# The low halves of the weights: from a subtraction on VectorE to an accumulating DMA, in a two-layer decoder trunk

## The chip, the cores and the metric

One core of one Trainium2 chip runs the whole program. The metric is the device time of one execution in microseconds (us); lower is better. The kernel before takes 1878.02 us (median of 2 runs, 1877.92 to 1878.12).

## The reference

Two layers over 512 tokens of width 1024, all in float32. Cut to the products, since all the weights that the change speaks of are used in them:

```python
for l in range(DEPTH):                       # 2
    h = rmsnorm(x, norm_mix_g[l])
    proj = h @ w_in[l]                       # 1024 x 7328: latents, q/k/v of three branches, gates
    y_a = latent attention (w_uq, w_ukv); y_b = stick-breaking attention; y_c = retention
    up = jnp.einsum('bsnw,nwd->bsnd', branches, w_branch[l])
    gates = jax.nn.sigmoid(gate_logits.reshape(B, S, N_BRANCH, D_MODEL))
    x = x + jnp.einsum('bsnd,bsnd->bsd', gates, up) @ w_out[l]
    h = rmsnorm(x, norm_mlp_g[l])
    x = x + jnp.square(jax.nn.relu(h @ w_up[l])) @ w_down[l]   # 1024 x 4096, 4096 x 1024
return rmsnorm(x, final_norm_g)
```

## The kernel before, in words

**Three products for one.** TensorE takes its operands as float32r, a rounded float32. To keep float32 accuracy each weight is used as a sum of two float32r parts, `hi` (the weight rounded) and `lo` (the rest), and so is each activation. A product is three matmuls per slice of 128 rows: hi by hi, hi by lo and lo by hi. `mm_T` (lines 460 to 465) writes transposed outputs, 128 columns by 512 tokens: its matmuls have the lines 462, 463 and 464, and only line 464 reads the `lo` part of a weight. `mm_N` (lines 467 to 476) writes natural outputs, 128 tokens by 256 columns.

**Units of weights.** The class `Weights` streams all weights in the order of their use. A chunk (mostly 1024 rows by 256 columns, 1 MB) is one DMA on SyncE's queue (SP) into one of two buffers `raw` (line 86). A chunk holds two units of 128 partitions by 1024 numbers (512 KB). `split` makes the two parts of a unit: ScalarE (ACT) rounds the unit into a buffer `whi`, and VectorE (DVE) subtracts that from the raw unit into a buffer `wlo` (both line 104). There are four pairs of these buffers, `whi0` to `whi3` and `wlo0` to `wlo3`, used in turn. `pump` splits up to two units ahead of the one that is taken; when the last unit of a chunk is split, the next chunk is asked for. There are 292 units of this plain form (`form` is None); the units of `w_uq` and `w_ukv` have forms of their own and are split in small pieces.

A unit holds either 8 slices of 128 columns (`plan_T` with 1024 rows: rows of 512 bytes in DRAM) or 4 slices of 256 columns (`plan_N`, and the branch weights: rows of 1 KB). Either way TensorE works on it for 24 matmuls of 512 columns or as much as that.

**Order of the work.** In each layer: inputs of the stick-breaking attention, latents, retention's values; then dense products with an attention in between (stick-breaking, latent, retention), since a driver interleaves the attentions' steps with the dense tiles; then the output projection (`w_out`, 8 units) and the MLP: four groups of 8 units of `w_up` and 8 of `w_down`. In the last group of the second layer the `w_down` tiles are computed in two halves of 256 tokens, so that its 8 units are streamed twice and each is used for half as long (16 half units, `put_last`, lines 1305 to 1321). The program's scheduler puts each engine's instructions in an order before the run; each engine then works in that order.

**GpSimd (POOL)** has little to do: the loads of constants, a power for each normalisation (lines 417 and 1032), the reload of the residual in front of the output projection (line 1229) and its store at the end of a layer (line 1300), which are DMAs on POOL's queue.

Of the kernel before, what the change touches and what calls it, by code (L numbers as in the profile page):

```python
# [10 lines left out]
F32 = mybir.dt.float32  # L11
R = mybir.dt.float32r
I32 = mybir.dt.int32
AF = mybir.ActivationFunctionType
ALU = mybir.AluOpType
# [6 lines left out]
EPS = 1e-6  # L22
# [6 lines left out]
GATE_RUN = (2, 2, 4)  # tiles of gates before their branch products  # L29
SC = 96.0**-0.5  # L30

# columns of w_in
# [3 lines left out]
# columns of the constant pack  # L36
# [8 lines left out]
# rows of the gain pack  # L45
# [3 lines left out]
class Weights:  # L49
    """Streams weight chunks from DRAM and splits each unit into two float32r parts."""  # L50
# [16 lines left out]
    def chunk(self, srcs, k, cols, units):  # L67
        """srcs: list of (dram view [p, k, c], column); units: list of (k0, k1, c0, c1, form)"""
        c = len(self.chunks)
        self.chunks.append((srcs, k, cols))  # L70
        self.left.append(len(units))
        for u in units:
            self.units.append((c, u))
# [18 lines left out]
    def split(self):  # L92
        nc = self.nc
        u = self.n_split
        c, (k0, k1, c0, c1, form) = self.units[u]
        s = self.free.popleft()
        self.slot[u] = s
        self.n_split += 1
        src = self.raw(c)[:, k0:k1, c0:c1]
        nk, w = k1 - k0, c1 - c0  # L100
        if form is None:
            hi = self.his[s][:, : nk * w].rearrange("p (k c) -> p k c", c=w)
            lo = self.los[s][:, : nk * w].rearrange("p (k c) -> p k c", c=w)
            self.last = (nc.scalar.copy(hi, src).ins, nc.vector.tensor_sub(lo, src, hi.bitcast(F32)).ins)  # L104
        elif form == "kv":
            # [head, key | value, 64] to [key | value, head, 64]
            hi = self.his[s][:, : nk * w].rearrange("p (k c) -> p k c", c=w)
            lo = self.los[s][:, : nk * w].rearrange("p (k c) -> p k c", c=w)
            for k in range(nk):
                a = src[:, k].rearrange("p (h s d) -> p h s d", s=2, d=64)  # L110
                b = hi[:, k].rearrange("p (s h d) -> p h s d", s=2, d=64)
                nc.scalar.copy(b, a)
                nc.vector.tensor_sub(lo[:, k].rearrange("p (s h d) -> p h s d", s=2, d=64), a, b.bitcast(F32))
        else:
            # a head's 96 columns of w_uq, as [64 | 32 | 32 swapped] or [32 | 32 swapped | 64]
            w = 128
            hi = self.his[s][:, : nk * w].rearrange("p (k c) -> p k c", c=w)
            lo = self.los[s][:, : nk * w].rearrange("p (k c) -> p k c", c=w)
            if form == 0:
                parts = [(0, 0, 96), (96, 80, 16), (112, 64, 16)]  # L120
            else:
                parts = [(64, 0, 64), (0, 64, 32), (32, 80, 16), (48, 64, 16)]
            for dst, at, n in parts:
                nc.scalar.copy(hi[:, :, dst : dst + n], src[:, :, at : at + n])
            for dst, at, n in parts:
                nc.vector.tensor_sub(
                    lo[:, :, dst : dst + n], src[:, :, at : at + n], hi[:, :, dst : dst + n].bitcast(F32)
                )
        self.views = getattr(self, "views", {})
        self.views[u] = (hi, lo)  # L130
        self.left[c] -= 1
        if self.left[c] == 0:
            self.dma()
# [20 lines left out]
def trunk_kernel(  # L154
# [15 lines left out]
    nc = tc.nc  # L170
# [7 lines left out]
    # ---------------------------------------------------------------- buffers  # L178
# [36 lines left out]
    # the functions of one table set are issued together  # L215
# [11 lines left out]
    def table(out, in_, func, **kw):  # L227
        """an activation from the table set in use"""
        i = nc.scalar.activation(out, in_, func, **kw).ins
        tc.add_manual_dep(i, phase["first"].name, order, reason="table set")  # L230
        phase["all"].append(i)

    # ---------------------------------------------------------------- driver
# [24 lines left out]
    def lend():  # L258
        """between attentions their banks serve the dense products"""
        dt.extend(spare)  # L260
# [8 lines left out]
    def evacuate(ps, fn):  # L269
        """run fn a little later; then ps may be written again"""  # L270

        def go():
            fn()
            waiting[id(ps)] = False

        defer(go)
# [38 lines left out]
    # ---------------------------------------------------------------- weights  # L315
# [3 lines left out]
    def plan_T(ap, width=256):  # L319
        """columns for transposed outputs, in units of 128"""  # L320
        v = planes(ap, 0)
        nk, cols = v.shape[1], v.shape[2]
        for c in range(0, cols, width):
            w = min(width, cols - c)
            step = 1024 // nk
            W.chunk([(v[:, :, c : c + w], 0)], nk, w, [(0, nk, a, a + min(step, w - a), None) for a in range(0, w, step)])
# [53 lines left out]
    # ---------------------------------------------------------------- constants  # L380
# [30 lines left out]
    # per-token statistics -----------------------------------------------------  # L411
    def to_rstd(ms, n, width, power=-0.5):
        """(ms / n + EPS) ** -0.5 for a [128, width] sum of squares"""
        a = tiny()
        nc.vector.tensor_scalar(a[:, :width], ms, 1.0 / n, EPS, op0=ALU.mult, op1=ALU.add)
        r = tiny()
        nc.gpsimd.tensor_tensor(r[:, :width], a[:, :width], mhalf[:, :width], op=ALU.pow)
        return r

    def token_sums(parts, n=NT):  # L420
        """sums over the partitions of all parts [128, 128 n] as [128 tokens, n]"""
        ps = rot(tt)
        for t in range(n):
            for i, a in enumerate(parts):
                nc.tensor.matmul(
                    ps[:, t : t + 1], a[:, t * P : (t + 1) * P], ones, start=(i == 0), stop=(i == len(parts) - 1)
                )
        return ps[:, :n]

    def row_sums(ps, sq):  # L430
        """sums over the partitions of sq, on every partition"""
        nc.tensor.matmul(ps, ones.to_broadcast([P, P]), sq, start=True, stop=True)

    def spread_to(ps, r, n=NT):
        """ps[:, token] = r[token] on every partition"""
# [10 lines left out]
    def split_to(hi, lo, src, g=None):  # L446
        """hi + lo = src * g"""
# [7 lines left out]
    # products -----------------------------------------------------------------  # L455
    def mm_T(ps, wh, wl, xs):
        """ps [128 columns, 512 tokens]; wh, wl: per k [128, 128]; xs: per k (hi, lo)"""
# [9 lines left out]
    def mm_N(ps, wh, wl, xs, t):  # L467
        """ps [128 tokens, N]; wh, wl: per k [128, N]"""
# [13 lines left out]
    class Later:  # L482
        """parts that a deferred step still has to emit"""
# [12 lines left out]
    def tile_T(xs, evac):  # L496
        """the next unit of 128 columns"""
# [7 lines left out]
    def tiles_N(n_units, evac):  # L505
        """the next units, stacked along k, for every token tile"""
# [10 lines left out]
    # ---------------------------------------------------------------- attention  # L517
    flatA = aT.rearrange("p r c -> p (r c)")

    def put_A(i, e, ps):  # L520
        """store the transposed blocks j = 0..i of query tile i and parity e"""
# [16 lines left out]
    def mask(z, i, m):  # L538
        """mask the diagonal blocks of query tile i"""
# [44 lines left out]
    def stick_breaking(qT, kT, v, yb):  # L584
        def first(p, i):
# [9 lines left out]
            # a[t] = sigmoid(z[t]) * product over t' > t of sigmoid(-z[t'])  # L595
# [58 lines left out]
    def retention(l, rq, rk, rv, rg, yc):  # L654
# [28 lines left out]
        def scores(t):  # L683
            # within the chunk, [key, query]
# [19 lines left out]
        def outputs(t):  # L704
            c = st[t]
            y = c["y"] = rot(zt)[:, 0]
            for p in range(PAIRS):
                b = slice(p * P, (p + 1) * P)
                if t:
                    # the state is zero between a pair's heads  # L710
# [9 lines left out]
            if t < NT - 1:  # L720
                # state after the chunk
# [25 lines left out]
        def norms(t):  # L747
            # group norm and gate, natural layout
# [15 lines left out]
            # 2 * silu  # L764
# [42 lines left out]
    # ---------------------------------------------------------------- set-up  # L807
    def setup():
# [35 lines left out]
        def tables():  # L844
            """cos and sin of positions * frequencies"""
# [30 lines left out]
            # per token: cos cos | -sin sin, over sqrt(96)  # L876
# [8 lines left out]
    # ---------------------------------------------------------------- a layer  # L885
    def layer(l, box):
        """box['next']: per-token rstd [128, 4] of the layer's input, once known"""
# [18 lines left out]
        # ---- stick-breaking inputs  # L906
        sq, sk, sv, yb = {}, {}, [get() for _ in range(NT)], {}

        def put_q(p):
            # per head [hi | hi], and the lo parts of the pair  # L910
# [13 lines left out]
        def put_k(p):  # L924
            # per head [hi | lo] or [lo | hi]
# [68 lines left out]
        # ---- latent vectors  # L994
# [26 lines left out]
        def stat_c(key, n):  # L1021
            # the latents still lack their token's rstd, which this folds in
# [39 lines left out]
        # ---- latent attention inputs  # L1062
# [67 lines left out]
        # ---- gates and branches  # L1130
# [58 lines left out]
        # ---- retention inputs, rotated  # L1189
# [45 lines left out]
        # ---- output projection, residual  # L1235
        stats = {}

        def new_x(m, g):
            """xm[m] is final: square it, split it"""
# [26 lines left out]
        # ---- MLP  # L1266
# [92 lines left out]
    # ---------------------------------------------------------------- run  # L1359
# [10 lines left out]
def _constants():  # L1370
    """tables that depend on shapes alone"""
# [29 lines left out]
def _layout(inputs):  # L1401
    """the program's inputs, in its order: x by columns, the gains and positions by partitions"""
# [29 lines left out]
```

## Time and profile before

| | us |
|---|---|
| median of 2 runs | 1878.02 |
| span of the profiled execution, first to last instruction | 1875.9 |
| TensorE (PE) busy in it | 1857.7 (99%) |
| VectorE (DVE) busy | 1064.1 (57%) |
| ScalarE (ACT) busy | 717.4 (38%) |
| GpSimd (POOL) busy | 42.5 (2%) |

The profile is of one execution with a span of 1875.9 us, 2.1 us under the median of the runs; that difference is what lies around the first and last instruction and between executions. Busy times of different engines lie beside each other and do not add up. A matmul's record lasts longer than the step to the next one, since matmuls are pipelined; the pace of TensorE is read from how many start in a stretch.

### The profile page before, as it was taken

To read this page: it belongs to the slowest core of one execution; us is meant where nothing else is said; L and a number is where in the kernel's file an instruction comes from. 1 tells how busy PE (TensorE), PEld (TensorE's weight loads), DVE (VectorE), ACT (ScalarE), POOL (GpSimd) and SP (SyncE) were. 2 spreads that over 40 slices of the span, in tenths; PEclk is the share of its full clock that TensorE was granted. 3 is DMA by queue.
4 is the path that set the end of the run, shared out by engine and by line. 5 is a ranking of instruction groups with operands and counts; after the bars stand their busy time and mean duration, and the time that the engine had idled before them with its cause. 6 is when DMAs were issued, how large, how long until landed. Compare 5 with 4: busy or idle time off the path is not lost.

```text
span 1875.9 us, 23563 instructions
## 1 busy us (share of the span) xinstructions
PE 1857.7 (99%) x9668; PEld 1533.4 (82%) x9668; DVE 1064.1 (57%) x1706; ACT 717.4 (38%) x1191; POOL 42.5 (2%) x57
## 2 busy tenths in 40 slices
PE   8999999999999999999999999999999999999998
PEld 7878877988888888888897787779888888888887
DVE  6775566577555444444638647646764654444456
ACT  5555444233243222323436454432333432323244
POOL 1000000001000000000000000000010000000000
PEclk9999999999999999999999999999999999999999
DMA  5220132122432322332423112221224233223324
GB/s 182 83 86 25 48 100 79 57 69 89 132 104 93 107 93 90 96 105 92 129 76 102 46 36 80 68 88 59 79 90 135 90 99 104 90 90 103 100 92 133
DMA packets 163980, 169.81 MB, mean 91 GB/s; under 512 B 5920, under 2 KB 160048, under 8 KB 163872
## 3 DMA queue, kind: packets, MB, share of 16 engines
q1 hardware_dynamic: 161360, 160.97, 27.4%
q0 software_dynamic: 2368, 7.30, 1.2%
q8 instruction: 76, 1.25, 0.3%
q14 instruction: 32, 0.26, 0.0%
q10 hardware_dynamic: 144, 0.03, 0.0%
HBM read 164.09 MB, written 4.19 MB: 90 GB/s over the span
## 4 chain that ended last, share of the span: by engine, by line
PE 98%; DMA 1%; DVE 1%; issue 0%; ACT 0%; POOLq 0%; SPq 0%; DVEq 0%
PE d L462 24%; PE d L464 24%; PE d L463 24%; PE d L474 4%; PE d L475 4%; PE d L476 4%; PE t L556 3%; PE t L548 2%; PE z L627 2%; PE z L593 1%; PE z L592 1%; DMA raw<-in_w_in_dram 1%; PE z L715 1%; PE z L476 1%; PE z L475 1%; PE z L474 1%
## 5 line engine op out<-in xcount | busy, mean ns | idle before, releaser
L104 ACT CAST whi<-raw 128x1024 fp32r<-128x1024 f32 (+1 forms) x292 | 305.9, 1049 | 672.5 <-PE d L463 552.9
L104 DVE TENSOR_TENSOR wlo<-raw,whi 128x1024 fp32r<-128x1024 f32 (+1 forms) x292 | 354.9, 1216 | 222.2 <-ACT whi L104 221.2
L462 PE MATMUL d<-xh,whi 128*128 128x512 f32 x1072 | 425.5, 397 | 7.0 <-ACT whi L104 7.0
L464 PE MATMUL d<-xh,wlo 128*128 128x512 f32 x1072 | 420.7, 393 | 0.6 <-DVE wlo L104 0.5
L463 PE MATMUL d<-xl,whi 128*128 128x512 f32 x1072 | 421.1, 393 | 0.1
L462 PE MATMUL d<-slot,whi 128*128 128x512 f32 (+1 forms) x960 | 368.5, 384 | 0.3 <-DVE slot L1309 0.3
L464 PE MATMUL d<-slot,wlo 128*128 128x512 f32 (+1 forms) x960 | 362.6, 379 | 0.0
L463 PE MATMUL d<-slot,whi 128*128 128x512 f32 (+1 forms) x960 | 362.1, 379 | 0.0
L462 PEld LDWEIGHTS d<-xh,whi 128*128 128x128 f32 x1072 | 201.9, 188 | 51.8 <-ACT whi L104 7.5
L464 PEld LDWEIGHTS d<-xh,wlo 128*128 128x128 f32 x1072 | 201.8, 188 | 44.5 <-DVE wlo L104 1.7
L463 PEld LDWEIGHTS d<-xl,whi 128*128 128x128 f32 x1072 | 202.0, 188 | 43.1 <-issue 2.4
L462 PEld LDWEIGHTS d<-slot,whi 128*128 128x128 f32 x960 | 180.3, 188 | 37.3 <-DVE slot L1309 0.5
L463 PEld LDWEIGHTS d<-slot,whi 128*128 128x128 f32 x960 | 180.3, 188 | 36.7 <-issue 0.5
L464 PEld LDWEIGHTS d<-slot,wlo 128*128 128x128 f32 x960 | 180.2, 188 | 36.9
L474 PE MATMUL d<-whi,xh 128*128 128x256 f32 x544 | 156.6, 288 | 0.0
L475 PE MATMUL d<-wlo,xh 128*128 128x256 f32 x544 | 155.1, 285 | 0.0
L476 PE MATMUL d<-whi,xl 128*128 128x256 f32 x544 | 154.9, 285 | 0.0
L1295 DVE TENSOR_TENSOR slot<-d,rkv_b 128x512 f32<-128x512 f32 x56 | 38.7, 691 | 150.0 <-PE d L464 150.0
L476 PEld LDWEIGHTS d<-whi,xl 128*128 128x128 f32 x544 | 104.1, 191 | 2.6 <-issue 2.6
L475 PEld LDWEIGHTS d<-wlo,xh 128*128 128x128 f32 x544 | 104.2, 191 | 2.4 <-issue 2.3
L474 PEld LDWEIGHTS d<-whi,xh 128*128 128x128 f32 x544 | 104.1, 191 | 1.7 <-issue 0.6
L449 ACT CAST slot<-slot 128x512 fp32r<-128x512 f32 x72 | 44.9, 624 | 88.2 <-DVE slot L1285 87.8
(204 smaller groups left out, 1865.9 us busy)
## 6 DMA issues: line engine op xcount, KB each, us to landing
raw<-in_w_in_dram SPq DMA_DIRECT2D x53, 1024.0 KB, 5.2
raw<-in_w_down_dram SPq DMA_DIRECT2D x36, 1024.0 KB, 5.1
raw<-in_w_up_dram SPq DMA_DIRECT2D x32, 1024.0 KB, 5.3
raw<-in_w_branch_dram SPq DMA_DIRECT2D x24, 512.0 KB, 3.4
raw<-in_w_out_dram SPq DMA_DIRECT2D x8, 1024.0 KB, 5.0
raw<-in_mla_w_uq_dram SPq DMA_DIRECT2D x4, 576.0 KB, 3.8
slot<-in_x_dram SPq DMA_DIRECT2D x8, 256.0 KB, 5.8
raw<-in_w_in_dram SPq DMA_DIRECT2D x4, 512.0 KB, 4.1
```

The costliest lines, as they stand in the source:

```text
L104: self.last = (nc.scalar.copy(hi, src).ins, nc.vector.tensor_sub(lo, src, hi.bitcast(F32)).ins)
L449: nc.scalar.copy(hi, src)
L462: nc.tensor.matmul(ps[:, :w], wh[k], h, start=(k == 0), stop=False)
L463: nc.tensor.matmul(ps[:, :w], wh[k], o, start=False, stop=False)
L464: nc.tensor.matmul(ps[:, :w], wl[k], h, start=False, stop=(k == n - 1))
L474: nc.tensor.matmul(ps, h, wh[k], start=(k == 0), stop=False)
L475: nc.tensor.matmul(ps, h, wl[k], start=False, stop=False)
L476: nc.tensor.matmul(ps, o, wh[k], start=False, stop=(k == n - 1))
L548: nc.tensor.transpose(ps[:, m * P : (m + 1) * P], a[:, e, j * P : (j + 1) * P], ident)
L556: nc.tensor.matmul(ps[e * 64 : (e + 1) * 64, j * P :], v[j][:, h * 64 : (h + 1) * 64], get_A(e, j), start=(j == 0), stop=(j == NT - 1), sk ...
L627: nc.tensor.matmul(z[:, e, :N], qT[h][:, i * P : (i + 1) * P], kT[h][:, :N], start=True, stop=True)
L1295: nc.vector.tensor_mul(t, ps, rstd2_b)
```

## The change

A plain unit whose chunk is read from one place in DRAM, other than the first six, gets its `lo` part in three steps in place of one: ACT writes the negated and rounded weights into `wlo` (new line 109), ACT writes the rounded weights into `whi` (line 110), and a DMA on POOL's queue reads the same weights once more from DRAM and adds them to what stands in `wlo` (line 111). The first six units and those read from two places (the columns of `w_in` that are packed with the rotary key) keep the subtraction on DVE. All other differences of the text are comments; later lines move down by 7.

```diff
         if form is None:
             hi = self.his[s][:, : nk * w].rearrange("p (k c) -> p k c", c=w)
             lo = self.los[s][:, : nk * w].rearrange("p (k c) -> p k c", c=w)
-            self.last = (nc.scalar.copy(hi, src).ins, nc.vector.tensor_sub(lo, src, hi.bitcast(F32)).ins)
+            srcs = self.chunks[c][0]
+            if u < 6 or len(srcs) > 1:
+                self.last = (nc.scalar.copy(hi, src).ins, nc.vector.tensor_sub(lo, src, hi.bitcast(F32)).ins)
+            else:
+
+                nc.scalar.activation(lo, src, AF.Copy, scale=-1.0)
+                nc.scalar.copy(hi, src)
+                nc.gpsimd.dma_start(lo, srcs[0][0][:, k0:k1, c0:c1], accum_op=ALU.add)
```

The order of ACT's instructions in the first layer's MLP, second group of `w_up` (`whi_86` is buffer 1 of the four, `slot` is the tile of hidden values that line 1284 reads out of PSUM and line 449 rounds), before:

```order
L104 CAST whi_86<-raw_84 128x1024
L1284 ACTIVATE slot_5084<-d_97 128x512
L449 CAST slot_5082<-slot_5084 128x512
L104 CAST whi_87<-raw_83 128x1024
L1284 ACTIVATE slot_5118<-d_98 128x512
```

and the same place now (lines 1291 and 456 are the former 1284 and 449; `wlo_90` and `wlo_91` belong to `whi_86` and `whi_87`):

```order
L110 CAST whi_86<-raw_84 128x1024
L1291 ACTIVATE slot_5174<-d_97 128x512
L109 ACTIVATE wlo_90<-raw_84 128x1024
L456 CAST slot_5172<-slot_5174 128x512
L110 CAST whi_87<-raw_83 128x1024
L1291 ACTIVATE slot_5209<-d_98 128x512
L109 ACTIVATE wlo_91<-raw_83 128x1024
```

The negated copy stands behind the rounding of the same unit and behind the read-out of a finished product; the rounding has kept its place.

On POOL's queue, from the end of the first layer's last gates to the start of its MLP, before:

```order
L1229 DMA slot_4250<-in_x_dram 128x512
L1229 DMA slot_4252<-in_x_dram 128x512
L1229 DMA slot_4254<-in_x_dram 128x512
L1300 DMA x_dram_131<-slot_4240 128x512
L1300 DMA x_dram_131<-slot_4242 128x512
```

and now (line 1236 is the former 1229):

```order
L1236 DMA slot_4316<-in_x_dram 128x512
L111 DMA wlo_89<-in_w_in_dram 128x8x128
L1236 DMA slot_4318<-in_x_dram 128x512
L111 DMA wlo_90<-in_w_in_dram 128x8x128
L111 DMA wlo_91<-in_w_branch_dram 128x4x256
L111 DMA wlo_92<-in_w_branch_dram 128x4x256
L111 DMA wlo_89<-in_w_out_dram 128x8x128
L111 DMA wlo_90<-in_w_out_dram 128x8x128
```

A queue that stood empty here now carries one DMA for each unit, 280 in all, and the reloads of the residual stand between them.

## Rows read from the trace of the kernel before

**Rows 1.** The page: busy us (share of the span) and instructions of each engine.

```profile
PE 1857.7 (99%) x9668; PEld 1533.4 (82%) x9668; DVE 1064.1 (57%) x1706; ACT 717.4 (38%) x1191; POOL 42.5 (2%) x57
```

**Rows 2.** The page: the chain that ended last, shares by engine.

```profile
PE 98%; DMA 1%; DVE 1%; issue 0%; ACT 0%; POOLq 0%; SPq 0%; DVEq 0%
```

**Rows 3.** The page: groups; busy us, mean ns of one, idle before, what ended it.

```profile
L104 ACT CAST whi<-raw 128x1024 fp32r<-128x1024 f32 (+1 forms) x292 | 305.9, 1049 | 672.5 <-PE d L463 552.9
L104 DVE TENSOR_TENSOR wlo<-raw,whi 128x1024 fp32r<-128x1024 f32 (+1 forms) x292 | 354.9, 1216 | 222.2 <-ACT whi L104 221.2
...
L464 PE MATMUL d<-xh,wlo 128*128 128x512 f32 x1072 | 420.7, 393 | 0.6 <-DVE wlo L104 0.5
```

**Rows 4.** Busy time by stretch: us, then each engine, granted clock, DMA share, GB/s.

```profile
723.00:811.00 88.00, 88.00 (x385) 71.91 (x384) 40.13 (x48) 25.80 (x32) 0.00 (x0) 1.00 0.30 96
1823.00:1868.00 45.00, 42.60 (x362) 42.23 (x361) 34.02 (x66) 26.46 (x44) 1.17 (x2) 1.00 0.40 131
```

**Rows 5.** Line 1309, the sixteen half units: duration min/median/max, first and last start.

```profile
L1309 DVE TENSOR_TENSOR slot<-d,rkv_b x16: 415/425/426, 1823.5 to 1865.0; 128x256 f32<-128x256 f32 x16
```

**Rows 6.** Timeline of ACT in the MLP: start us, us, operation, idle before and releaser.

```profile
693.75 1.06 ACT L104 CAST whi<-raw 128x1024 fp32r<-128x1024 f32 x1 [1.88 <-PE d L463]
694.71 0.59 ACT L1284 ACTIVATE slot<-d 128x512 f32<-128x512 f32 x1
696.70 0.62 ACT L449 CAST slot<-slot 128x512 fp32r<-128x512 f32 x1 [1.40 <-DVE slot L1285]
699.18 1.05 ACT L104 CAST whi<-raw 128x1024 fp32r<-128x1024 f32 x1 [1.86 <-PE d L463]
```

**Rows 7.** DMA, 100 to 106 us: one chunk of 1 KB rows; packets, MB, share.

```profile
GB/s 0 0 34 82 130 109 123 96 191 212 348 382 389 389 375 389 396 382 382 382 389 382 396 375 348 239 62 7 0 0 0 0 0 0 0 0 0 0 0 0
...
q1 hardware_dynamic: 1040, 1.05, 57.0%
```

**Rows 8.** DMA, 76 to 83 us: one chunk of 512-byte rows; last row KB and us to landing.

```profile
GB/s 0 0 0 0 0 0 0 0 0 47 97 64 105 208 272 290 336 348 345 351 322 182 29 0 0 0 0 0 0 0 0 0 0 0 0 0 0 0 0 0
...
q1 hardware_dynamic: 1040, 0.52, 28.3%
...
raw<-in_w_in_dram SPq DMA_DIRECT2D x1, 512.0 KB, 3.8
```

**Rows 9.** Groups of POOL: busy us, mean ns of one, idle before, releasers.

```profile
L1229 POOL DMA_DIRECT2D slot<-in_x_dram x8 | 4.4, 546 | 45.5 <-DVE slot L1150 26.9 <-PE d L464 16.2 <-DVE slot L1155 2.4
...
L825 POOL DMA_DIRECT2D zeta<-in_consts_dram x1 | 0.5, 537 | 0.0
...
L823 POOL DMA_DIRECT2D decay<-in_consts_dram x1 | 0.5, 536 | 0.0
```

**Rows 10.** Timeline of ACT in the half units.

```profile
1835.40 1.06 ACT L104 CAST whi<-raw 128x1024 fp32r<-128x1024 f32 x1 [0.61 <-PE d L463]
1836.44 0.42 ACT L1311 ACTIVATE slot<-slot 128x256 f32<-128x256 f32 x1
1836.89 0.51 ACT L1312 ACTIVATE slot<-slot,gain 128x256 f32<-128x256 f32 x1
```

## The prediction

> **What bounds the kernel now.** I read the engines' busy times first, then the chain that ended last, then the groups of the line that changes, then single stretches. TensorE is busy for 1857.7 of 1875.9 us [rows 1] and is 98% of the chain [rows 2], so 18.2 us is all that any other engine's relief could give back. The subtraction that goes, line 104 on DVE, costs 280 x 1.216 = 340 us of DVE time, but the matmul that reads its result waited 0.5 us for it in the whole run [rows 3]. It lies beside TensorE. The question is only whether the new way to `lo` keeps pace with TensorE.
>
> That pace is strict. In the MLP 385 matmuls start in 88.00 us [rows 4], 0.2286 us each, so a unit (24 matmuls) lasts 5.49 us, with no idle time at all. The sixteen half units at the end follow each other at (1865.0 - 1823.5) / 15 = 2.77 us [rows 5]. On ACT the rounding of a unit waits each time until TensorE has finished with the buffer [rows 6]: four buffers in turn, so it runs as early as it can, three units (16.5 us) before its use. Latency is covered there; throughput is what counts.
>
> **The change part by part.**
>
> *Removed on DVE:* 340 us off the path, worth 0.
>
> *Added on ACT:* 280 passes like the rounding, 1.05 us each [rows 3], 294 us on an engine with 717 us of work [rows 1]. In the MLP a unit then takes 1.05 + 1.05 + 0.59 + 0.62 = 3.31 us of ACT [rows 6] against 5.49: hidden, and the order puts the new pass into the 1.4 us that ACT waited for DVE. In the half units it is 1.05 + 1.05 + 0.42 + 0.51 = 3.03 us [rows 10] against 2.77: 0.26 us over, on some 13 units 3 us, if nothing slower stands there.
>
> *Added on the DMA engines:* 512 KB per unit, read once more. First what is there: a chunk of 1 KB rows holds 16 engines for 57.0% of 6 us = 3.42 us [rows 7], 1.71 us per unit. A 512 KB chunk of 512-byte rows takes 28.3% of 7 us = 1.98 us [rows 8]; the MLP's units are of that row size. No row of this trace shows an accumulating transfer. From below it costs no more than a plain one in a loaded stretch: 0.524 MB at 345 GB/s [rows 8] = 1.5 us, when the read of `lo` and the add lie beside the read from DRAM. From above each 512-byte row costs two 1 KB rows: 6.84 us. The nearest row is the plain 512-byte one, taken twice, because two operands must be read: 3.96 us. I take that. With the chunk's load a unit needs 1.71 + 3.96 = 5.67 us of all 16 engines, against 5.49 us of TensorE. So the DMA engines just overtake TensorE: 0.18 us per unit.
>
> The Trainium skill (Collectives: The Full Stack, The bandwidth ceiling) says that a reduce inside the DMA reads two sources and runs at about half the rate of a copy, 1.93 measured. No run here shows it yet. By it the estimate would be 3.82 in place of 3.96 us and 5.53 us per unit, practically level with TensorE.
>
> *Added on POOL:* 280 DMA instructions. A DMA instruction there takes 0.54 us whether it moves 4 or 512 KB, but every one has 128 rows [rows 9]; the MLP's have 1024. From below 0.54 us; if all of it were per row, 8 x 0.54 = 4.3 us; if the reads of `lo` are listed too, 8.7 us. I take at most 4.3, which lies beside the 5.67 us of the DMA engines. Queued behind one another are also the reloads of the residual, which wait for free tiles (45.5 us in all [rows 9]). The one before the last gates' units waits for a branch tile that is 2.5 units (13.7 us) ahead of the gate whose DMA stands behind it, so I put it at 0.
>
> *Latency, where the cover is short:* from the end of a unit to a ready `lo`: on ACT 1.05 + 0.59 + 1.05 = 2.7 us by the new order, 0.54 on POOL, 3.8 for a plain landing [rows 8] and 1.98 for the second read: 9.0 us (before: 1.05 + 1.22 = 2.3). Bounds are 7.0 (plain) and 15.2 (8.7 on POOL). The lead is 16.5 us in the MLP, but only one unit, 5.49, behind the product that takes three units at once, and three small `w_uq` units of nine matmuls, 6.2 us, ahead of the first gates. That is 3.5 + 2.8 us per layer, 12.6 us for two; by the bounds 5 and 37.
>
> *Sum against the profiled execution:*
> - 136 whole units without an attention beside them (16 of `w_out`, 64 + 56 of the MLP) x 0.18 = 24.5 us;
> - half units: the fourth is ready 9.0 us after the stage starts, the last twelve steps later, 9.0 + 12 x 5.67 + 2.77 = 79.8 us against 16 x 2.77 = 44.3: 35.5 us;
> - short leads: 12.6 us.
>
> Together 72.6: a span of 1948.5 us. The runs lie 2.1 us above the span, so 1951 us, 3.9% slower. About 2% can be told from no change here.
>
> **The rivals.**
>
> *It hides.* If the second read is cheap, or packets flow as fast as in the middle of a loaded stretch (389 GB/s for 1 KB rows [rows 7], 345 for 512-byte rows [rows 8]), a unit needs 1.35 + 2 x 1.52 = 4.4 us, under 5.49. The whole units then cost nothing; only the half units pay, 9.0 + 12 x 4.4 + 2.77 = 64.6, 20 us more, and the short leads 12.6: 1911 us. At the plain price (3.69 us per unit, latency 7.0) it is 10 + 5 us: 1893 us. For it: those rates are real rows, and DMA stood at 30% in the MLP [rows 4]. Against: no margin is left for an add that costs more than its bytes. It decides below some 4.7 us per unit. This is the case "not slower" by over 2%.
>
> *POOL becomes the bound.* If an instruction lists 1024 rows to read, 1024 to add to, and all of the 0.54 us is per row, POOL needs 8.7 us per 512-byte unit and works them off one by one: 136 x 3.17 = 431 us, half units 15.2 + 12 x 8.66 + 2.77 - 44.3 = 78 us, short leads 37: 2424 us. A DMA at its upper bound (1.71 + 6.84 = 8.55 us) gives nearly the same, 2405. For it: 1024 rows are eight times what POOL listed at once before. Against: the 0.54 us surely has a fixed part. The Trainium skill (DMA: Bandwidth & Descriptors, Anatomy of one DMA) calls descriptor generation small and says that many descriptors can be emitted before the cost shows; no run here shows it, since the row count never varies.
>
> *Worse still:* each accumulated row waits for its own read, over 10 us per unit: above 2600 us.
>
> *Faster:* all of TensorE's idle time is 18.2 us [rows 1], 1%; even with all of it gone it is 1860 us. More than 2% would need quicker matmuls, for which nothing speaks.
>
> **How the numbers follow.** Forecast (5.2 to 7 us per unit, 1920 to 2150 us) 0.40; it hides (1890 to 1915) 0.32; a bound near 8.7 (2250 to 2450) 0.20; worse 0.06; faster 0.02. The range reaches from the bottom of the hiding case to the top of the POOL case, 1889 to 2440. Slower by over 2% is 0.40 + 0.20 + 0.06 = 0.66, within 2% 0.32, faster 0.02.
>
> **What would show it.** Right: in the MLP matmuls of line 464 wait for `wlo` and the releaser is a DMA, units follow at 5.6 to 5.8 us, DMA share there is near 1.0, POOL's instruction stays under 5 us, the last stage takes about 80 us. Hiding: 5.49 us per unit still, DMA share below 0.85, and only the end is longer. POOL: its instructions last 6 us and more, back to back, with DMA share well below 1. If units wait and neither POOL nor the DMA engines are full, it is the latency of the chain copy, issue, landing that I mis-sized. A granted clock below 1.00 in the MLP would mean that the waits themselves slow the matmuls, which I have not priced: in the half units it stayed at 1.00 with TensorE busy for 42.6 of 45 us [rows 4].

## The result, and the profile after

The changed kernel takes 1910.23 us (median of 2 runs, 1908.88 to 1911.58) against 1878.02 before: 1.0173 times as long, with a 95% interval of 1.0154 to 1.0192. That is 32 us slower, where the forecast was 73. One of the ten executions of e3 below took 4733.49 us, two and a half times the others; nothing on record says why, and its ratio rests on the other nine.

| | before, us | after, us |
|---|---|---|
| median of 2 runs | 1878.02 | 1910.23 |
| span of the profiled execution | 1875.9 | 1907.1 |
| mean granted clock of TensorE | 0.998 | 0.993 |
| last sum of `put_out` in layer 0 starts at | 583.2 | 586.1 |
| last sum of `put_out` in layer 1 starts at | 1509.3 | 1520.9 |
| first of the sixteen half units at | 1823.5 | 1835.1 |
| last of the sixteen half units at | 1865.0 | 1896.4 |

The last four rows are start times of the same DVE instructions in both programs (lines 1251 and 1309, now 1258 and 1316), and they show where the time went: 2.9 us are lost by the output projection of layer 0, 8.7 more (11.6 - 2.9) by that of layer 1, nothing in either MLP up to the half units (1835.1 - 1823.5 is 11.6 still), and 19.8 in the half units (31.4 - 11.6).

The page of the kernel after: busy us of each engine, answering to [rows 1], and the groups of the new lines, answering to [rows 3, 9]. The columns are engine, operation, tiles, count | busy us, mean ns of one | idle time of the engine before them, and what ended it.

```profile
PE 1868.3 (98%) x9668; PEld 1542.0 (81%) x9668; DVE 751.2 (39%) x1426; ACT 965.7 (51%) x1471; POOL 461.6 (24%) x337
...
L110 ACT CAST whi<-raw 128x1024 fp32r<-128x1024 f32 x280 | 294.0, 1050 | 585.4 <-PE d L470 331.3
L471 PE MATMUL d<-xh,wlo 128*128 128x512 f32 x1072 | 423.2, 395 | 8.4 <-DMA wlo<-in_w_in_dram 7.9
L471 PE MATMUL d<-slot,wlo 128*128 128x512 f32 (+1 forms) x960 | 366.3, 383 | 12.0 <-DMA wlo<-in_w_down_dram 12.0
L109 ACT ACTIVATE wlo<-raw 128x1024 fp32r<-128x1024 f32 x280 | 295.5, 1055 | 46.0 <-PE d L482 32.9
...
L111 POOL DMA_DIRECT2D wlo<-in_w_up_dram x64 | 98.7, 1542 | 259.5 <-ACT wlo L109 225.2
```

DVE has lost 313 us of work and ACT gained 248, and neither moves the end. What is new stands at the right of the two matmul groups of line 471: TensorE now waits for a DMA, 7.9 us in all for units of `w_in` and 12.0 for units of `w_down`. Before, the same matmuls waited 0.5 us [rows 3]. A DMA instruction of 1024 rows takes 1.54 us on POOL, which is busy for 24% of the span.

The list of TensorE's waits says how often and how long (us in all, times, longest):

```profile
PE d L471 <- DMA wlo<-in_w_down_dram: 12.0, 6, 3.3
PE d L471 <- DMA wlo<-in_w_in_dram: 7.9, 2, 6.2
```

Only eight waits, and not one for a unit of `w_up`, `w_out` or `w_branch`. If every whole unit were late by a little there would be more than a hundred. The same 88 us of the MLP as in [rows 4], and then three stretches of the half units: us, busy time of PE, PEld, DVE, ACT and POOL, granted clock, DMA share, GB/s.

```profile
723.00:811.00 88.00, 88.00 (x386) 71.91 (x385) 22.16 (x32) 40.06 (x48) 24.58 (x16) 1.00 1.08 191
...
1845.00:1855.00 10.00, 7.47 (x48) 7.09 (x48) 2.43 (x6) 5.20 (x10) 3.09 (x2) 0.83 1.28 240
1855.00:1863.00 8.00, 5.49 (x24) 5.20 (x24) 0.51 (x3) 2.03 (x4) 1.55 (x1) 0.57 1.35 212
1863.00:1875.00 12.00, 11.35 (x95) 11.18 (x96) 4.24 (x13) 9.74 (x15) 5.35 (x4) 1.00 1.31 244
```

In the MLP 386 matmuls start in 88 us, against 385 before: the pace of 5.49 us per unit is untouched, although the DMA share went from 0.30 to 1.08. A share of 1.08 is the first thing to stop at: it cannot be a share of a resource that is then full. In the half units it reaches 1.35, TensorE is idle for part of the time, and in two of the three stretches its granted clock is below 1.00.

The sixteen half units, answering to [rows 5] (duration min/median/max, first and last start):

```profile
L1316 DVE TENSOR_TENSOR slot<-d,rkv_b x16: 415/425/426, 1835.1 to 1896.4; 128x256 f32<-128x256 f32 x16
```

They follow each other at (1896.4 - 1835.1) / 15 = 4.09 us in the mean, where it was 2.77. The steps are uneven, since the first three units were ready when they were wanted. The accumulations for the fourth and for the last of the sixteen on POOL, each with its time from issue to landing:

```profile
1832.37 1.54 POOL L111 DMA_DIRECT2D wlo<-in_w_down_dram  x1 [3.92 <-ACT wlo L109]
DMA to landing us min/median/max: 8.2/8.2/8.2
...
1883.34 1.54 POOL L111 DMA_DIRECT2D wlo<-in_w_down_dram  x1 [2.88 <-ACT slot L1318]
DMA to landing us min/median/max: 9.9/9.9/9.9
```

They land at 1840.6 and 1893.2 us, twelve steps of 4.38 us. The bytes say nearly the same. From 1837 to 1890 us, 53 us with a DMA share above 1, they carried (packets, MB, share of each queue):

```profile
q0 software_dynamic: 12873, 6.49, 97.3%
q1 hardware_dynamic: 5314, 5.24, 34.4%
```

That is 6.49 / 0.524 = 12.4 accumulations, one per 4.28 us. The DMA view of the stretch 700 to 711 us, in the MLP, shows what the engines do there: GB/s in 40 equal slices, then packets, MB and share of each queue (q0 is POOL's, the accumulation; q1 is SP's, the loads). The last line is q0 again, from 705.5 to 709 us, where no other queue has a packet.

```profile
GB/s 52 125 175 305 372 369 279 231 287 328 346 328 298 223 199 149 164 171 171 184 182 181 186 184 155 73 102 119 143 155 168 184 173 184 182 182 182 138 37 0
...
q0 software_dynamic: 2110, 1.06, 78.1%
q1 hardware_dynamic: 1040, 1.05, 32.3%
...
q0 software_dynamic: 1066, 0.54, 123.7%
```

Where only the accumulation runs, 512 KB flow at some 182 GB/s: 0.524 MB / 182 = 2.88 us per unit. Each packet, though, lasts 0.781 x 11 us x 16 / 2110 = 65 ns, and 1024 rows of 65 ns on 16 engines would be 4.2 us. Both are true only if an engine has more than one packet under way, and the last line says so directly: one queue alone reads a share of 1.24. So durations cannot be added up to an occupancy. By the rates, the bytes of the 53 us above are 6.49 MB / 182 + 5.24 MB / 389 = 35.7 + 13.5 = 49 us, not far from all of the stretch. The loads show the same on a smaller scale, and did so before: by duration a 1 MB chunk was 3.42 us of 16 engines, at its plateau of 389 GB/s it needs 1.05 / 389 = 2.70 [rows 7].

### The profile page after: what moved, and what is told of

The parts are those of the page before. It is cut to its first block, busy times and chain, and to the rows that moved or that the text cites. A ratio compares the mean times of both kernels' runs of the same rounds, so it can differ in the third digit from the quotient of the medians.

```text
span 1907.1 us, 24123 instructions
## 1 busy us (share of the span) xinstructions
PE 1868.3 (98%) x9668; PEld 1542.0 (81%) x9668; DVE 751.2 (39%) x1426; ACT 965.7 (51%) x1471; POOL 461.6 (24%) x337
## 5 line engine op out<-in xcount | busy, mean ns | idle before, releaser
L110 ACT CAST whi<-raw 128x1024 fp32r<-128x1024 f32 x280 | 294.0, 1050 | 585.4 <-PE d L470 331.3
L109 ACT ACTIVATE wlo<-raw 128x1024 fp32r<-128x1024 f32 x280 | 295.5, 1055 | 46.0 <-PE d L482 32.9
L111 POOL DMA_DIRECT2D wlo<-in_w_in_dram x104 | 152.2, 1463 | 627.6 <-ACT wlo L109 570.2
L469 PEld LDWEIGHTS d<-slot,whi 128*128 128x128 f32 x960 | 183.0, 191 | 38.6 <-issue 2.0
L470 PEld LDWEIGHTS d<-slot,whi 128*128 128x128 f32 x960 | 182.9, 190 | 36.8 <-issue 1.0
L111 POOL DMA_DIRECT2D wlo<-in_w_down_dram x72 | 111.2, 1544 | 250.2 <-ACT wlo L109 216.7
L111 POOL DMA_DIRECT2D wlo<-in_w_up_dram x64 | 98.7, 1542 | 259.5 <-ACT wlo L109 225.2
L1292 DVE TENSOR_TENSOR slot<-slot 128x512 f32<-128x512 f32 x64 | 44.2, 691 | 209.4 <-ACT slot L1291 209.4
```

The lines of the kernel that those rows point to most:

```text
L109: nc.scalar.activation(lo, src, AF.Copy, scale=-1.0)
L111: nc.gpsimd.dma_start(lo, srcs[0][0][:, k0:k1, c0:c1], accum_op=ALU.add)
L469: nc.tensor.matmul(ps[:, :w], wh[k], h, start=(k == 0), stop=False)
L470: nc.tensor.matmul(ps[:, :w], wh[k], o, start=False, stop=False)
L1292: nc.vector.tensor_mul(h, h, h)
```

## The experiments

The theory after this reading: what counts on the DMA engines is bytes at the rate of a loaded stretch, 2.88 us for the accumulation and 1.35 for the unit's load, 4.2 us per unit together. That is below 5.49, so whole units hide it; it shows where TensorE needs less time per unit (the half units) and where the lead is short (the first units behind the product that takes three at once). The rival is the prediction's own sum, durations added up, by which whole units pay as well. Smaller rivals are the latency of the chain and ACT in the half units. The kernel before, run beside them on the same chips, took 1877.63 us (first four) and 1877.91 (last three).

**e1: the sixteen half units keep the subtraction.**

```diff
-            if u < 6 or len(srcs) > 1:
+            if u < 6 or len(srcs) > 1 or u >= len(self.units) - 16:
```

> The last 16 units (the half units) get the subtraction on VectorE back, everything else as in the changed kernel. Theory A (the loss sits in two places where units are wanted faster than the DMA engines deliver them; the half units are one): the half units follow each other at 2.8 us again in place of 4.1, and 19.8 us go: 1890 us. Theory B (the second read and the extra ACT passes slow the whole kernel a little, in proportion to the units): 16 of 280 units are 6% of 32 us, 2 us: 1908 us.

Measured: 1891.59 us, 1.0073 times before (1.0056 to 1.0090). The half units and the remaining waits of line 471:

```profile
L1316 DVE TENSOR_TENSOR slot<-d,rkv_b x16: 414/425/426, 1837.3 to 1878.8; 128x256 f32<-128x256 f32 x16
```

```profile
PE d L471 <- DMA wlo<-in_w_in_dram: 8.7, 2, 6.1
```

The pace is 2.77 us again (41.5 / 15), and with sixteen units out of 280 changed back some 18 of the 32 us are gone. The other 264 units cost the remaining 14.

**e2: the three units that are split together behind the three-unit product keep it**, in each layer.

```diff
-            if u < 6 or len(srcs) > 1:
+            if u < 6 or len(srcs) > 1 or u in (10, 11, 12, 162, 163, 164):
```

> Three units in each layer, those split together behind the product that holds three weight units at once, get the subtraction back. Theory A (the other place is the burst behind that product): the 6.2 us wait for an accumulating DMA in the second layer and the half clock behind it go, 9 to 11 us less than the changed kernel: 1900 us. Theory B (proportional): 6 of 280 units, under 1 us: 1909 us.

Measured: 1899.13 us, 1.0117 (1.0102 to 1.0132). The wait for `w_in` at line 471 has left the list; that for `w_down` stays, and so do the half units' 4.27 us (64.1 / 15):

```profile
PE d L471 <- DMA wlo<-in_w_down_dram: 13.6, 7, 2.7
```

```profile
L1316 DVE TENSOR_TENSOR slot<-d,rkv_b x16: 415/425/426, 1825.0 to 1889.1; 128x256 f32<-128x256 f32 x16
```

The half units start at 1825.0 in place of 1835.1. So six units were the cause of most of the time lost ahead of the half units, 10.1 of 11.6 us.

**e3: both.** 258 units still accumulate.

```diff
-            if u < 6 or len(srcs) > 1:
+            if u < 6 or len(srcs) > 1 or u >= len(self.units) - 16 or u in (10, 11, 12, 162, 163, 164):
```

> Both of these together: 258 units still go by the accumulating DMA. Theory A: 1878 to 1881 us, the kernel before within its noise, although 135 MB are still read twice. Theory B: 92% of the loss stays, about 1907 us.

Measured: 1878.89 us, 1.0007 (0.9997 to 1.0017): nothing is left of the 32 us. The MLP's stretch is as busy as ever on the DMA engines:

```profile
723.00:811.00 88.00, 88.00 (x385) 71.99 (x384) 22.16 (x32) 40.06 (x48) 24.67 (x16) 1.00 1.08 191
```

This is the best version with the accumulation in it, and it is no faster than the kernel before: TensorE is the bound of both.

**e4: a plain DMA in place of the accumulating one.** The low parts then hold the whole weights, so this is a probe of the time alone.

```diff
-                nc.gpsimd.dma_start(lo, srcs[0][0][:, k0:k1, c0:c1], accum_op=ALU.add)
+                nc.gpsimd.dma_start(lo, srcs[0][0][:, k0:k1, c0:c1])
```

> The changed kernel with a plain DMA in place of the accumulating one: the same rows, bytes from DRAM, queue and waits, but nothing is added, so the low parts hold the whole weights and the output is another one. If reading the second operand is what a row of 512 bytes pays (66 ns in the changed kernel against 29 ns for a plain load), rows fall to about 30 ns, the half units are bound by ACT at about 3.0 us each, the wait in the second layer shrinks to about 2 us, and the run takes 1884 to 1890 us. If POOL's queue or the ACT passes cost the time, it stays at 1905 to 1910 us.

Measured: 1889.71 us, 1.0065 (1.0045 to 1.0085). POOL's group of `w_in` (1463 ns each when it accumulates), the half units and the largest wait:

```profile
L111 POOL DMA_DIRECT2D wlo<-in_w_in_dram x104 | 87.3, 840 | 672.6 <-ACT wlo L109 614.3
```

```profile
L1316 DVE TENSOR_TENSOR slot<-d,rkv_b x16: 416/425/426, 1829.8 to 1876.3; 128x256 f32<-128x256 f32 x16
```

```profile
PE d L471 <- DMA wlo<-in_w_in_dram: 3.2, 1, 3.2
```

The half units now follow at 3.10 us. That is near ACT's 3.03 per unit [rows 10], but that ACT sets the pace now is not shown: from 1834 to 1865 us ACT stood idle for 5.4 us, 2.3 of them for a chunk's load. So some 20 of the 32 us go with the add (with it, too, POOL's instruction is longer), and 12 with moving the bytes once more and with the longer way of a unit.

One part of the expectation failed: the rows did not fall to 30 ns. From 704 to 708 us, with no other queue beside them, POOL's plain packets last 0.685 x 4 us x 16 / 1040 = 42 ns, and in the half units 1.255 x 26 us x 16 / 8080 = 65 ns. POOL's queue in the two windows (704 to 708 and 1836 to 1862 us):

```profile
q0 software_dynamic: 1040, 0.52, 68.5%
...
q0 software_dynamic: 8080, 4.08, 125.5%
```

Packets of 65 ns stand in the half units of e4 beside 318 GB/s of both queues together, where the changed kernel moved 222. A packet's duration does not tell how fast the bytes flow.

**e5: half a unit more of traffic.** After each accumulation, half of `hi` is stored to a scratch tile in DRAM. One more added line, which makes the sixteen scratch tiles, is left out of the cut here and in e6; later lines move down by two here and by three there.

```diff
                 nc.gpsimd.dma_start(lo, srcs[0][0][:, k0:k1, c0:c1], accum_op=ALU.add)
+                nc.sync.dma_start(self.copy[(1 * u + 0) % 16][:, :512], self.his[s][:, :512].bitcast(F32))
```

> The changed kernel, and for every unit with an accumulating DMA one more plain DMA on SyncE's queue: half of the rounded unit (256 KB) is stored into scratch memory in DRAM, which nobody reads. Theory A (engines work on packets of several queues side by side; what counts is bytes per second in a loaded stretch: 2.9 us for the accumulation at 182 GB/s, 1.35 for the load at 390, 0.7 for the store): 4.9 us per unit, still under TensorE's 5.49, so whole units in the MLP keep 5.49 us and only the half units grow from 4.1 to 4.7 us: about 1920 us. Theory C (packet durations add up, 5.94 us per unit already, the MLP stands at its limit): 0.7 us on each of 136 whole units and more at the end, over 2000 us.

Measured: 1938.17 us, 1.0321 (1.0300 to 1.0342).

```profile
723.00:811.00 88.00, 88.00 (x385) 71.88 (x385) 22.03 (x33) 39.93 (x49) 24.67 (x16) 1.00 1.21 239
```

```profile
L1318 DVE TENSOR_TENSOR slot<-d,rkv_b x16: 414/424/425, 1855.3 to 1927.8; 128x256 f32<-128x256 f32 x16
```

```profile
PE d L473 <- DMA wlo<-in_w_in_dram: 20.3, 5, 11.2
```

At a share of 1.21 the MLP still starts 385 matmuls in 88 us: with a quarter more bytes the whole units are still hidden, which a sum of durations excludes (4.2 for the accumulation and 1.7 for the load are over 5.49 already without the store). The half units follow at 72.5 / 15 = 4.83 us in the mean; bytes at rates say 4.23 + 0.67 (0.26 MB at 389 GB/s) = 4.9. The total misses the expectation by 18 us, because the short leads at the layers' starts grew far more than thought, from 7.9 to 20.3 us of waits, and the half units start 20 us later than in the changed kernel (1855.3 against 1835.1). The accumulation that TensorE waits for in layer 1 lands 14.9 us after its issue here and 9.9 in the changed kernel.

**e6: two stores of a whole unit.**

```diff
                 nc.gpsimd.dma_start(lo, srcs[0][0][:, k0:k1, c0:c1], accum_op=ALU.add)
+                nc.sync.dma_start(self.copy[(2 * u + 0) % 16][:, :1024], self.his[s][:, :1024].bitcast(F32))
+                nc.sync.dma_start(self.copy[(2 * u + 1) % 16][:, :1024], self.his[s][:, :1024].bitcast(F32))
```

> The same with two stores of the whole rounded unit, 1 MB of writes per unit. Theory A: 2.9 + 1.35 + 2.7 = 6.9 us per unit, over 5.49, so now the MLP is bound by the DMA engines at about 6.9 us per unit, the half units by the same: 136 x 1.4 + 16 x 2.8 = 235 us above the changed kernel, 2120 to 2200 us. If the MLP stays at 5.49, the DMA engines carry more than I take from the loaded stretches, and something else sets the pace of the half units.

Measured: 2296.19 us, 1.2227 (1.2203 to 1.2252). A stretch of the MLP and the two largest waits:

```profile
940.00:1030.00 90.00, 75.26 (x277) 56.65 (x276) 15.91 (x23) 25.26 (x29) 18.51 (x12) 0.89 1.19 280
```

```profile
PE d L474 <- DMA wlo<-in_w_down_dram: 88.4, 42, 8.9
PE d L474 <- DMA wlo<-in_w_up_dram: 75.2, 41, 4.1
```

Now whole units pay, and this is what my forecast's world would have looked like: dozens of waits in the MLP for `w_up` and `w_down`. A unit takes 24 x 90 / 277 = 7.8 us; the rates added up gave 6.9. The size was missed: this mixture of loads, adds and stores moves 280 GB/s, so 2.1 MB need 7.5 us, and the granted clock is at 0.89 in this stretch. That the DMA engines alone set the 7.8 us is argued, not shown: an accumulation for `w_up` now lands 20.9 us after its issue (median), so that a buffer spends 20.9 of the 31 us (4 x 7.8) between two uses on that transfer alone, and no run had more than four buffers. The share, 1.19, is lower than e5's 1.21, where nothing was bound: the share does not tell whether the DMA engines are full.

**e7: the negated copy on DVE**, which takes 1.05 us per unit off ACT.

```diff
-                nc.scalar.activation(lo, src, AF.Copy, scale=-1.0)
+                nc.vector.tensor_scalar_mul(lo, src, -1.0)
```

> The negated copy is made by VectorE in place of ScalarE; the accumulating DMA stays. ACT then has 1.98 us per half unit in place of 3.03, and a unit's low part is ready some 1 to 2 us earlier. Theory A (the DMA engines set the pace of the half units): they stay at 4.0 to 4.1 us, 1905 to 1911 us in all, the wait in the second layer is 1 us shorter at most. Rival D (ACT, or the time until one of the four buffers is ready again, sets it): the half units come at 3.4 to 3.7 us and the run falls to 1898 to 1903 us.

Measured: 1912.34 us, 1.0181 (1.0164 to 1.0198).

```profile
L1316 DVE TENSOR_TENSOR slot<-d,rkv_b x16: 415/424/426, 1838.9 to 1900.7; 128x256 f32<-128x256 f32 x16
```

4.12 us per half unit, as with ACT's copy. The total is just above the expected 1905 to 1911 us, and the longest wait for `w_in` fell from 6.2 to 4.4 us, more than the 1 us expected, without a gain in the total. ACT does not set the half units' pace, and a way that is 1.05 us shorter on ACT does not quicken it; the DMA engines set it, as e4 and e5 say from the other sides.

## Why the prediction was wrong

The direction was right (slower), the likeliest case was not: the forecast was 1951 us with 0.66 on slower by over 2%, and what happened is the rival "It hides", 1911 us, which had 0.32. The measured time lies inside the range.

**The step that failed** is "With the chunk's load a unit needs 1.71 + 3.96 = 5.67 us of all 16 engines, against 5.49 us of TensorE." The sizes in it were fair: measured by its packets the accumulation is 4.2 us, about twice the plain transfer of 1.98, as the step took it. What was wrong is the plus sign and the word "of all 16 engines". Packets of one queue and of two queues overlap on an engine: the shares add to 1.08 in the MLP and 1.35 in the half units. The rate of a loaded stretch is what counts, and by it the unit needs 2.88 + 1.35 = 4.2 us; in the half units the engines carried one accumulation per 4.28 us, and whole units, at 5.49 us, paid nothing. I had read those rates [rows 7, 8] and used them in the rival only.

The Trainium skill (Collectives: The Full Stack, The bandwidth ceiling) found the reduce of a collective at 1 / 1.93 of a copy's rate and lays that to its two source reads. The trace agrees with the ratio where rates are compared: 182 GB/s for the accumulation, against 345 for a plain load of 512-byte rows [rows 8], is 1 / 1.9. That two reads are the reason no run here shows.

Term by term:

- *Whole units, 24.5 us:* measured 0. The MLP keeps 5.49 us per unit, and by e3 all 258 units outside the two critical places together cost 1.3 us (by its interval -0.6 to 3.2).
- *Half units, 35.5 us:* measured 19.8. The place and the form of the sum were right, the time per unit was not: counted from 2.77 us before the first half unit's sum (1835.1), the fourth unit's accumulation lands after 8.3 us (9.0 in the forecast) and the last one after 60.9, twelve steps of 4.38 us in place of 5.67. The rival had 4.4 and its 20 came out.
- *Short leads, 12.6 us:* measured 2.9 + 8.7 = 11.6, though not by the parts that I named. I had 3.5 us behind the three-unit product and 2.8 between the `w_uq` units and the first gates, in each layer. The second is 0 in both: no wait of that place is in the list. The first is a wait of 1.7 us in layer 0 and of 6.2 us in layer 1. That the sum is near 12.6 is luck.
- *ACT, POOL, DVE:* the new copy takes 1.055 us (forecast 1.05) and is hidden; POOL's instruction takes 1.54 us, near the lower of the bounds 0.54 and 8.7, so the rival of POOL as the bound fell, and the residual's reloads between the units cost nothing. The subtraction's 340 us on DVE were worth nothing, as said.

Why layer 1 loses more shows in the timelines of ACT, POOL and TensorE, first layer 0, then layer 1 (start us, us, operation, idle before and what ended it):

```profile
57.84 1.06 ACT L109 ACTIVATE wlo<-raw 128x1024 fp32r<-128x1024 f32 x1
59.21 1.55 POOL L111 DMA_DIRECT2D wlo<-in_w_in_dram  x1 [6.90 <-ACT wlo L109]
68.10 0.50 PE L471 MATMUL d<-xh,wlo 128*128 128x512 f32 x1 [1.69 <-DMA wlo<-in_w_in_dram]
...
990.60 1.06 ACT L109 ACTIVATE wlo<-raw 128x1024 fp32r<-128x1024 f32 x1 [4.91 <-PE z L482]
991.96 1.55 POOL L111 DMA_DIRECT2D wlo<-in_w_in_dram  x1 [14.50 <-ACT wlo L109]
993.96 1.53 POOL L111 DMA_DIRECT2D wlo<-in_w_in_dram  x1 [0.46 <-ACT wlo L109]
995.75 1.53 POOL L111 DMA_DIRECT2D wlo<-in_w_in_dram  x1 [0.25 <-ACT wlo L109]
1001.89 0.80 PE L471 MATMUL d<-xh,wlo 128*128 128x512 f32 x1 [6.18 <-DMA wlo<-in_w_in_dram]
```

Three units become free at once, so three accumulations are issued within 4 us, with a chunk's load beside them. In layer 1 they land 9.9, 14.2 and 15.2 us after their issue (the median of `w_in` is 8.0), but TensorE waited for the first alone; that one takes 8.8 us in layer 0. From the start of the negated copy to the landing it is 10.2 us in layer 0 and 11.3 in layer 1, where I had 9.0 (in layer 1, 1.4 us to the issue and 9.9 to the landing, where I had 2.7 and 6.3). TensorE comes to the unit 8.6 us after that start in layer 0 and 5.1 in layer 1, where I had 5.49 for both. So the latency was mis-sized by 1.2 and 2.3 us, and most of the difference between the layers is the lead: in layer 1 TensorE has only a few matmuls left of the unit that it already holds when the three-unit product ends, since twenty of them ran ahead of the product's last tile (984.83 to 989.17 us; two in layer 0, at 54.25 and 54.48).

TensorE's busy time and clock in the four stretches from 990 to 1010 us, columns as above:

```profile
990.00:995.00 5.00, 4.59 (x26) 3.71 (x27) 1.12 (x2) 4.40 (x5) 2.59 (x2) 1.00 0.23 56
995.00:1000.00 5.00, 0.71 (x2) 0.27 (x2) 3.80 (x12) 4.91 (x12) 2.03 (x2) 0.93 1.24 249
1000.00:1005.00 5.00, 3.11 (x7) 2.48 (x8) 0.00 (x0) 1.95 (x2) 1.53 (x1) 0.50 1.27 237
1005.00:1010.00 5.00, 5.00 (x20) 3.67 (x18) 0.00 (x0) 0.98 (x1) 0.00 (x0) 0.89 1.37 208
```

TensorE stands for 6.2 us, and the matmuls behind the wait run at half the clock (0.50, the level of 1.2 GHz). Three lines of TensorE's timeline behind the wait:

```profile
1002.91 0.63 PE L470 MATMUL d<-xl,whi 128*128 128x512 f32 x1
1003.34 0.63 PE L471 MATMUL d<-xh,wlo 128*128 128x512 f32 x1
...
1006.24 0.40 PE L469 MATMUL d<-xh,whi 128*128 128x512 f32 x1
```

They step by 0.43 us in place of 0.23. The ten steps from 1001.89 to 1006.24 take 4.35 us in place of 2.3 and add some 2 us to the wait: 8.2 of the 8.7 us that layer 1 lost. In layer 0 the wait is 1.7 of the 2.9 us; what the rest is was not looked for. The prediction named this ("the waits themselves slow the matmuls, which I have not priced"), for the MLP; it happened at the layers' starts and in the half units, where the clock reads 0.57 to 0.83 behind the waits. What the clock costs inside the half units was not separated from the wait by a run of its own.

Of the signs that were to show the hiding case, "5.49 us per unit still" and "only the end is longer" came true; "DMA share below 0.85" did not (1.08), for the reason above: the sign rested on the same wrong reading of the share.

## What to carry to other kernels

Before a transfer is added beside others, work out bytes over the GB/s of a loaded stretch, kind by kind, and compare the sum with the time that the consumer takes per unit (leave some room: in e6 the sum was 6.9 us and the bytes took 7.5); packet durations, and the DMA share made of them, are an upper bound in which overlapping packets count twice, and a share near or above 1 does not yet mean that anything waits. Then look for the few places where the consumer is faster than its usual pace or the lead is short, and price these with the lead that each really has and with the latency beside other transfers, since a change that is hidden in 258 of 280 units still costs what the other 22 make of it. Work taken off an engine that nothing waits for is worth nothing, so only those places decide.

## What the runs showed of the hardware

- The share of the DMA engines in the profile goes above 1: 1.08 in the MLP, 1.35 in the half units, and 1.21 (e5) with no matmul of the MLP late, against 1.19 (e6) where the MLP waits dozens of times. One queue alone reached 1.24.
- An accumulating DMA from DRAM onto a tile with rows of 512 bytes flows at 182 GB/s and lands 512 KB in about 8 us. On POOL its instruction takes 1.54 us for 1024 rows, the plain one in e4 0.875 (`w_up`), and those with 128 rows 0.54 [rows 9]. The Trainium skill (DMA: Bandwidth & Descriptors, Anatomy of one DMA) calls the time to generate descriptors small. If the longer instruction is that time, the trace agrees in part: eight times the rows cost 1.6 times the time when plain and 2.9 times when accumulating, and POOL is still idle for 76% of the span.
- Loads, accumulations and stores together reached 280 GB/s in e6, less than the single rates add up to (2.1 MB in 7.5 us in place of 6.9). Why was not tried.
- A wait of 6.2 us halved TensorE's granted clock for the matmuls behind it, so that the wait and the slower steps together cost some 8 us.
